# The end stage of a two-layer decoder trunk: the order of four compute engines laid out by hand, one gate half or partial product in each slot

## The chip, the cores and the metric

One NeuronCore of a Trainium2 chip runs the whole program in one launch. The metric is the device time of that launch in microseconds; the median of three runs is given. The engines are TensorE (PE, with its weight loads as PEld), VectorE (DVE), ScalarE (ACT), GpSimd (POOL) and SyncE (SP), which issues all DMAs that matter here.

## What is computed

Two pre-norm residual layers over 2048 tokens of width 1024, and a final RMSNorm. Layer 0 mixes by gated linear attention, layer 1 by dilated sliding-window attention: six heads of 128, three (window, dilation) groups each, whose outputs are combined by a softmax over their log-sum-exps. Each layer has a cross-attention into 256 memory tokens and a SiLU gate of the branch width. The end stage of the program holds the end of layer 1:

```python
    for g, (window, dil) in enumerate(DIL_GROUPS):
        ...
        o, lse = dilated_group(q, k, qkv[:, :, 2], window, dil)
    wts = jax.nn.softmax(jnp.stack(lses, axis=0), axis=0)
    o = jnp.einsum('gbth,gbthd->bthd', wts, jnp.stack(outs, axis=0).astype(jnp.float32))
...
        branch = jnp.concatenate([mix, mem_o], axis=-1) * jax.nn.silu(gate)
        x = x + branch @ w_out[i]
    return rmsnorm(x, final_norm_w)
```

## The kernel before

**Precision.** A product in float32 is made of three matmuls (`mm3`, L180 to L183): each operand is split into a high part (a cast on ACT) and a low part (the difference, on DVE or POOL), and hi x hi, hi x lo and lo x hi are summed in PSUM. The attention probabilities are split by `split_P` (L171 to L178): ACT makes the high half, POOL (L175) the low half, and SP issues a transposing DMA (L176).

**Main loop.** Layer 1 has 18 head passes (6 heads by 3 groups). The loop of `NS` = 144 slots takes eight slots a pass. In a slot s PE makes the scores of slot s - 10 (`att_scores`), the product of probabilities and values of slot s - 13 (`att_pv`, so three slots after its scores) and one 512-wide projection of q or k (`proj_t`, 24 matmuls). DVE adds the mask and takes the row maximum (L1257), ACT exponentiates (L1268). Every four slots the rotary embedding runs (`rope_a`, `rope_b`, `rope_c`: shuffle, two products, a sum, a fold, a subtraction and eight copies). Inside this loop the order of PE, DVE, ACT and POOL is the program's own (`manual_schedule` with all four engines); SP's order is always the planner's.

**Chunks of a head.** When a head's three groups are done, its statistics are transposed (`att_stats`), stored (`stats_out`), read back (`prep_load`), turned into weights (`prep_mix`, `prep_out`), read again as rows broadcast to all partitions (`item_fb`, into the tile fb), and applied to the group outputs (`item_og` loads them; `item_mul`, one DVE and two POOL products; `item_sum`, three DVE instructions). The result of a chunk of 512 tokens is one of eight 128-wide pieces of the branch, kept in DRAM (brd). The steps of the first five heads are spread over slots by `mixes`.

**End stage.** It follows the loop and has slots x = 0 to 13 and then 16 output blocks of 128 tokens. In the slots the last 10 scores and 13 value products run, the four chunks of the last gate column (`gate_half`, eight halves of 12 matmuls, then the SiLU by exponential, logarithm and exponential on ACT), the end of the fifth head, the four chunks of the sixth head (h = 5), whose piece is not stored but split into b5, and the split of w_out (four raw loads of 1 MB, `wo_split`) into wo0, wo1 and wo2. An output block multiplies the branch (seven pieces loaded and split into bhl, the eighth from b5) by w_out: `f_main` makes the seven pieces' part of one 512-wide half, P1 or P2, into a PSUM bank, `f_fin` adds the eighth, adds the residual x1 on DVE (L1651) and squares on ACT, and `f_end` applies the final norm (L1667) and stores.

In this stage only PE's order is the program's. The planner orders DVE, ACT, POOL and SP by its own estimates. Of PE's order: gate halves 0, 1 in slot 0, 2, 3 in slot 1, then one a slot to slot 5; P1 of block 0 in slot 7, of block 1 in slot 9, P2 of both in slots 11 and 12, P1 of block 2 in slot 13; all four chunks of h = 5 are loaded at x = 4, 6, 8, 10 and multiplied at x = 6, 8, 10, 12.

**PSUM.** `mm_bank` rotates over three banks (ps_mm twice, ps_x); scores have two banks (ps_g), value products one of ps_o and one of ps_tr in turn.

Of the kernel before, what the change touches and what calls it, by code (L numbers as in the profile page):

```python
# [36 lines left out]
def trunk(ctx, tc, a, out):  # L37
# [1389 lines left out]
    def mixes(s):  # L1427
# [25 lines left out]
    with ExitStack() as c5:
        c5.enter_context(tc.manual_schedule(engines={getattr(mybir.EngineType, e_) for e_ in MANUAL}))
        chunk = None
        for s in range(NS):
# [54 lines left out]
            mixes(s)  # L1511
            wcur = wnext
# [7 lines left out]
    def wo_raw(j, t):  # L1520
        SY.dma_start(t, a["w_out"][1, :, j * 256:(j + 1) * 256].rearrange("(k p) n -> p k n", p=P))
        return t

    def wo_split(raw, hi, lo):
        A.activation(out=hi, in_=raw, func=AF.Copy)
        V.tensor_tensor(out=lo, in0=raw, in1=hi.bitcast(F32), op=ALU.subtract)

    last = hds[NH - 1]
# [4 lines left out]
    def gate_half(x):  # L1533
# [7 lines left out]
        if hf == 1:  # L1541
            gate_silu(gt.pop(c), c)
# [6 lines left out]
    raws = {0: wo_raw(0, tl(stg, [P, KT, 256], F32, "stg"))}  # L1549
    wo0 = [tl(wp, WSH, F32R, "w") for _ in range(4)]  # L1550
    its, fbs, pre, b5s = {}, {}, {}, {}
    for x in range(14):
        if x < 10:
            scores(NS - 10 + x)
        if x < 13:
            pv(NS - 13 + x)
        if x == 4:
            stats_out(*att_stats(hds.pop(NH - 2), 0))
        if x < 4:
            for f in todo.pop(NS + x, []):  # L1560
                f()
            mixes(NS + x)
        if x == 7:
            f_main(fs[0], P1)
        if x == 9:
            f_main(fs[1], P1)
        for y in ((0, 1), (2, 3), (4,), (5,), (6,), (7,))[x] if x < 6 else ():
            gate_half(y)
        c, odd = divmod(x - 3, 2)
        if 0 <= c < 4 and not odd:  # L1570
            stats_out(*att_stats(last, c))
        c, odd = divmod(x - 4, 2)
        if x == 1:
            brs = [t[:, 0:(KT - 1) * P].rearrange("p (k n) -> p k n", k=KT - 1) for t in rope]
            for y in range(2):
                load_br(y)
        if 0 <= c < 4:
            if not odd:
                pre[c] = prep_load(5, c)
                its[c] = item_og(5, c)  # L1580
            else:
                prep_out(*prep_mix(pre.pop(c)))
                fbs[c] = item_fb(5, c)
        c, odd = divmod(x - 6, 2)
        if 0 <= c < 4 and not odd:
            it = its.pop(c), fbs.pop(c), last["osb"].pop(c)
            item_mul(*it)
            sg = item_sum(*it)
            b5s[c] = tl(vp, [P, 2, 512], F32R, "v")
            wo_split(sg, b5s[c][:, 0], b5s[c][:, 1])  # L1590
        if x in (1, 2):
            kh = x - 1
            wo_split(raws[0][:, 4 * kh:4 * kh + 4], wo0[kh], wo0[2 + kh])
# [3 lines left out]
        if x in (4, 5):  # L1597
            ks = slice(4 * (x - 4), 4 * (x - 3))
            wo_split(raws[1][:, ks], wo1[0][:, ks], wo1[1][:, ks])
        if x == 4:  # L1600
            raws[2] = wo_raw(2, tl(vp, [P, KT, 256], F32, "v"))
        if x == 6:
            raws[3] = wo_raw(3, tl(stg, [P, KT, 256], F32, "stg"))
        if x == 5:
            ch.close()
            f0 = c4.enter_context(pool("f0", 1, "right"))
            fp = c4.enter_context(pool("fp", 3, "right"))
            wo2 = [tl(f0, [P, KT, 512], F32R, nm) for nm in ("wh2", "wl2")]
            x1v = x1_d.rearrange("(b p) d -> b p d", p=P)
            ov = out.rearrange("(b p) d -> b p d", p=P)  # L1610
            fw = tl(wp, [P, D], F32, "w")
            SY.dma_start(fw, bcast_row(a["final_norm_w"], D))

            bhls = [tl(f0, [P, 2, KT - 1, P], F32R, f"bhl{y}") for y in range(2)]

            def load_b(p_, br=True):
                if br:
# [4 lines left out]
                return dict(p=p_, x=xt, b=bhls[p_ % 3], ss=tl(sp, [P, 4], F32, "ss4"), n=0, t={},
                            e=tl(pk, [P, D], BF16, "pm"))

            def wcol(k, lo, c0, n):
# [4 lines left out]
                return wo2[lo][:, k, c0 - 512:c0 - 512 + n]  # L1630

            def f_main(d, parts, t=None):
                t = mm_bank() if t is None else t
                d["t"][parts[0]] = t
                lo_ = parts[0][0]
                for c0, n in parts:
                    for k in range(KT - 1):
# [4 lines left out]
            def f_fin(d, parts):
                t = d["t"].pop(parts[0])
                lo_, hi_ = parts[0][0], parts[-1][0] + parts[-1][1]
                b5 = b5s[d["p"] // 4]
                ts = slice(d["p"] % 4 * P, (d["p"] % 4 + 1) * P)
                for c0, n in parts:
                    mm3(t[:, c0 - lo_:c0 - lo_ + n], b5[:, 0, ts], b5[:, 1, ts], wcol(5, 0, c0, n), wcol(5, 1, c0, n),
                        False, c0 + n == hi_)
                cs = slice(lo_, hi_)  # L1650
                V.tensor_tensor(out=d["x"][:, cs], in0=t[:, :hi_ - lo_], in1=d["x"][:, cs], op=ALU.add)  # L1651
                A.activation(out=d["e"][:, cs], in_=d["x"][:, cs], func=AF.Square,
                             accum_out=d["ss"][:, d["n"]:d["n"] + 1])
                d["n"] += 1

            def f_mm(d, parts):
                f_main(d, parts)
                f_fin(d, parts)

            def f_end(p_, d, w):  # L1660
                tot = tl(sp, [P, 1], F32, "ss")
                V.tensor_reduce(out=tot, in_=d["ss"][:, :d["n"]], axis=AX.X, op=ALU.add)
                r = rstd_of(tot, 1, D)
# [93 lines left out]
```

## Time and profile before

| What | Value |
|---|---|
| median of three runs | 2592.41 us (2585.83 to 2594.94) |
| the profiled execution's own time | 2593.54 us |
| its span | 2591.8 us |
| PE busy | 2497.6 us, 96% of the span |
| DVE, ACT, POOL busy | 1576.0, 1345.9, 582.6 us |
| first scores of the end stage | at 2332.61 us |

Times in the profile are counted from the start of the span. A row of the timeline gives the start, the duration, the engine, the line, the operation, the tile that is written and those that are read; square brackets give the idle time before the instruction and what ended it. A helper's line stands for every caller (L181 to L183 are all the split products; L1526 is the low half of every `wo_split`), so the tile names tell which product it is: ps_g<-k,q are scores, ps_o or ps_tr<-pt,v value products, ps_mm or ps_x<-h2T,w projections and gates, and products with w, q, k, wh or wl as weights and bhl, q or v as the other operand output blocks.

### The profile page before, as it was taken

The numbers are of one execution on the slowest core, as the hardware profiler recorded it, in microseconds if no ns is written. First come the engines' busy times: TensorE is split into PE (matmuls) and PEld (weight loads), VectorE is DVE, ScalarE is ACT, GpSimd is POOL, SyncE is SP. The second block draws the span as 40 slices with busy tenths as digits, with TensorE's granted clock in tenths as the row PEclk, the third lists the DMA queues.
The fourth block names the chain that finished last, engine by engine and source line by source line (L and its number), as shares of the span: only waits on it lengthen the run. The fifth ranks groups of instructions, "written<-read, shape, count | busy, mean of one in ns | idle before, by whom it ended". The sixth has DMA issues, their size and how long they took to land. (4 is left out here: it accounts for less than half of the span.)

```text
span 2591.8 us, 45023 instructions
## 1 busy us (share of the span) xinstructions
PE 2497.6 (96%) x17033; PEld 1678.4 (65%) x17033; DVE 1576.0 (61%) x3582; ACT 1345.9 (52%) x2944; POOL 582.6 (22%) x471
## 2 busy tenths in 40 slices
PE   7999999899999899999999999999999999996899
PEld 6979999788889744444544455555555555554798
DVE  7346444565875765765655455676776767677642
ACT  7346543643454545755555455565556556556222
POOL 0000000010210223455543022233232323223100
PEclk9999999899999999999999999999999999998999
DMA  6242111345544554568674314365573846659642
GB/s 211 84 130 100 62 52 74 118 109 121 155 135 125 147 171 126 152 164 188 164 200 125 118 49 115 95 176 152 140 192 101 196 122 173 153 142 250 183 153 83
DMA packets 563312, 356.55 MB, mean 138 GB/s; under 512 B 383555, under 2 KB 495637, under 8 KB 562709
## 3 DMA queue, kind: packets, MB, share of 16 engines
q1 hardware_dynamic: 563092, 353.66, 50.1%
q8 instruction: 133, 2.18, 0.4%
q14 instruction: 87, 0.70, 0.1%
HBM read 185.74 MB, written 95.86 MB: 109 GB/s over the span
## 5 line engine op out<-in xcount | busy, mean ns | idle before, releaser
L181 PE MATMUL ps_mm<-h2T,w 128*128 128x512 f16 x1112 | 422.7, 380 | 7.0 <-ACT w L851 5.7
L183 PE MATMUL ps_mm<-h2T,w 128*128 128x512 f16 x1112 | 422.4, 380 | 0.3 <-DVE w L855 0.3
L182 PE MATMUL ps_mm<-h2T,w 128*128 128x512 f16 x1112 | 422.5, 380 | 0.0
L181 PE MATMUL ps_mm<-w,hT 128*128 128x256 f16 (+1 forms) x1408 | 389.0, 276 | 3.3 <-ACT v L491 1.3
L182 PE MATMUL ps_mm<-w,hT 128*128 128x256 f16 (+1 forms) x1408 | 387.9, 276 | 0.0
L183 PE MATMUL ps_mm<-w,hT 128*128 128x256 f16 (+1 forms) x1408 | 386.5, 276 | 0.4 <-DVE hT L385 0.4
L183 PEld LDWEIGHTS <-w 128*128 128x128 f16 x1952 | 191.3, 98 | 232.4 <-issue 1.9
L181 PEld LDWEIGHTS <-w 128*128 128x128 f16 x1952 | 191.3, 98 | 217.4 <-ACT w L851 5.9
L182 PEld LDWEIGHTS <-w 128*128 128x128 f16 x1952 | 191.3, 98 | 217.0 <-issue 9.0
L175 POOL TENSOR_TENSOR ph<-pm,ph 128x512 f16<-128x512 f32 (+2 forms) x144 | 165.8, 1151 | 638.2 <-ACT ph L174 441.5
L181 PE MATMUL ps_x<-h2T,w 128*128 128x512 f16 x552 | 209.2, 379 | 1.4 <-DVE c L1079 1.4
L183 PE MATMUL ps_x<-h2T,w 128*128 128x512 f16 x552 | 209.2, 379 | 0.0
L182 PE MATMUL ps_x<-h2T,w 128*128 128x512 f16 x552 | 209.2, 379 | 0.0
L1268 ACT ACTIVATE pm<-pm,st,cols 128x256 f32<-128x256 f32 (+1 forms) x288 | 156.2, 544 | 79.8 <-DVE st L1261 78.2
L175 POOL TENSOR_TENSOR stg<-mp,stg 128x512 f16<-128x512 f32 x16 | 18.6, 1160 | 743.7 <-DMA ogd<-og 456.9
L1257 DVE CUSTOM_DVE_ANT_0 pm<-ps_g,mw 128x256 f32<-128x256 f32 (+1 forms) x288 | 93.0, 359 | 103.8 <-PE ps_g L183 103.0
L181 PEld LDWEIGHTS <-hT 128*128 128x128 f16 x1408 | 139.4, 99 | 24.7 <-issue 5.4
L182 PEld LDWEIGHTS <-hT 128*128 128x128 f16 x1408 | 139.2, 99 | 23.5 <-issue 4.5
L183 PEld LDWEIGHTS <-hT 128*128 128x128 f16 x1408 | 139.8, 99 | 18.6 <-DVE hT L385 0.7
L1217 ACT ACTIVATE rx<-rw 128x512 f16<-128x512 f32 x36 | 33.9, 941 | 115.7 <-DVE rw L1216 115.7
L1201 ACT ACTIVATE rx<-ps_mm 32x512 f32<-32x512 f32 x96 | 56.1, 584 | 58.1 <-DVE k L1227 26.1
L174 ACT ACTIVATE ph<-pm 128x512 f16<-128x512 f32 (+2 forms) x144 | 77.2, 536 | 4.5
(502 smaller groups left out, 5995.3 us busy)
## 6 DMA issues: line engine op xcount, KB each, us to landing
stg<-in_w_in_b SPq DMA_DIRECT2D x80, 256.0 KB
v<-vd SPq DMA_DIRECT2D x72, 256.0 KB
fb<-fd SPq DMA_DIRECT2D x24, 768.0 KB
od<-osb SPq DMA_DIRECT2D x68, 256.0 KB
og<-od SPq DMA_DIRECT2D x68, 256.0 KB
x<-in_x SPq DMA_DIRECT2D x32, 512.0 KB
stg<-in_w_in_b SPq DMA_DIRECT2D x24, 512.0 KB
vd<-vo SPq DMA_DIRECT2D x48, 256.0 KB
```

The source lines that it names most:

```text
L174: A.activation(out=hi, in_=src, func=AF.Copy)
L175: G.tensor_tensor(out=lo, in0=src, in1=hi, op=ALU.subtract)
L181: PE.matmul(o, sh, mh, start=first, stop=False)
L182: PE.matmul(o, sh, ml, start=False, stop=False)
L183: PE.matmul(o, sl, mh, start=False, stop=last)
L1201: A.activation(out=X[r0:r0 + 32, :], in_=t[0:32, :], func=AF.Copy)
L1217: A.activation(out=fold(X.bitcast(F16)[:, 0:512], g), in_=perm(W, g), func=AF.Copy, scale=SQ)
L1257: V.tensor_tensor_reduce(out=pm[:, at:at + w * P], in0=s[:, at:at + w * P], in1=masks["mw" if w == 2 else "mf"], scale=1.0, scalar=NEG, op ...
L1268: A.activation(out=p_, in_=p_, func=AF.Exp, scale=sc, bias=st[:, jc + jj:jc + jj + 1], accum_out=st[:, ns + jc + jj:ns + jc + jj + 1])
```

## The change

The end stage gets `manual_schedule` for PE, DVE, ACT and POOL, so that the program's order is now the order on all four. SP stays with the planner. Within this order:

- Slots 0 to 7 hold one gate half each, slots 8 to 11 P1 of blocks 0 to 3, slots 12 and 13 P2 of blocks 0 and 1. These six partial products take three banks of mm_bank, both of ps_g and ps_o.
- `gate_silu` is parted: the exponentials follow the gate's second half, the final product (`gate_out`) comes a slot later. `wo_split` is parted into `wo_hi` and `wo_lo`, the low half mostly a slot later. Statistics of h = 5 are transposed in slots 5, 7, 9, 11 and stored a slot later.
- The first raw block of w_out is asked for at the end of slot 143; its split stands in slots 0 and 1, after the rope of the loop. Raw 2 and raw 3 are loaded in slots 6 and 8 and split in slots 8, 9 and 10, 11.
- Only chunk 0 of h = 5 is handled in the slots (load 6, weights 7 and 8, product 11, sum 12). Chunk 1 is loaded in slot 12 and multiplied after block 2; chunks 2 and 3 follow in blocks 3 to 7 and 7 to 11.
- `f_end` of a block comes after P1 of the next. The split of block p + 1 (from block 4 on) stands in block p.
- Buffers: four group outputs of the last head have their own tiles (osb, rw, rx, sg2); the x1 tiles lie where q and k were; the split branch tiles lie in old v and w tiles and in a new pool; b5 lies in the staging tile.

```diff
+    def gate_e(t):
+        e = tl(bk, [P, 512], F32, "rx")
+        V.tensor_scalar(out=e, in0=t, scalar1=gneg5, scalar2=87.0, op0=ALU.mult, op1=ALU.min)
+        A.activation(out=e, in_=e, func=AF.Exp)
+        A.activation(out=e, in_=e, func=AF.Ln, bias=one1)
+        A.activation(out=e, in_=e, func=AF.Exp, scale=-1.0)
+        return e
+
+    def gate_out(t, c, e):
         sg = tl(bk, [P, 512], F32, "sg2")
-        silu(t, 512, [wg5["inv"][0]], [gneg5], sg, bk, "rx")
+        V.scalar_tensor_tensor(out=sg, in0=t, scalar=wg5["inv"][0], in1=e, op0=ALU.mult, op1=ALU.mult)
         SY.dma_start(sg_d[5][:, c * 512:(c + 1) * 512], sg)
...
             mixes(s)
+            if s == NS - 1:
+                raws = {0: wo_raw(0, tl(stg, [P, KT, 256], F32, "stg"))}
...
-    def wo_split(raw, hi, lo):
+    def wo_hi(raw, hi, lo):
         A.activation(out=hi, in_=raw, func=AF.Copy)
+
+    def wo_lo(raw, hi, lo):
         V.tensor_tensor(out=lo, in0=raw, in1=hi.bitcast(F32), op=ALU.subtract)
+    c4.enter_context(tc.manual_schedule(engines={getattr(mybir.EngineType, e_) for e_ in MANUAL}))
...
+    last["own"] = [(gk, [P, 512], F32, "osb")] + [(bk, [P, 512], F32, nm) for nm in ("rw", "rx", "sg2")]
...
+    def split_later(x, *a_):
+        wo_hi(*a_)
+        later(NS + x + 1, wo_lo, *a_)
...
     for x in range(14):
+        now[0] = x
         if x < 10:
             scores(NS - 10 + x)
         if x < 13:
             pv(NS - 13 + x)
+        for f in todo.pop(NS + x, []):
+            f()
         if x < 4:
             mixes(NS + x)
+        if x in (5, 7, 9, 11):
+            later(NS + x + 1, stats_out, *att_stats(last, (x - 5) // 2))
+        if x < 8:
+            gate_half(x)
+        elif x < 12:
+            f_main(fs[x - 8], P1, bank(ps_g) if x == 11 else None)
+        else:
+            f_main(fs[x - 12], P2, bank(ps_g if x == 12 else ps_o))
+        if x == 3:
+            later(NS + 4, stats_out, *att_stats(hds[NH - 2], 0))
+        if x == 0:
+            load_br(0)
+            load_br(1)
+        if x < 2:
+            w_split(x, 0, x)
         if x == 2:
             raws[1] = wo_raw(1, tl(stg, [P, KT, 256], F32, "stg"))
             wo1 = [tl(qp, [P, KT, 256], F32R, nm) for nm in ("q", "k")]
         if x in (4, 5):
+            w_split(x, 1, x - 4)
...
         if x == 6:
+            raws[2] = wo_raw(2, tl(stg, [P, KT, 256], F32, "stg"))
+            last_load(0)
+        if x == 6:
+            b_hi(0)
+            later(NS + 7, b_lo, 0)
+        if x == 7:
+            last_mix(0)
+            b_hi(1)
+        if x == 8:
             ch.close()
             f0 = c4.enter_context(pool("f0", 1, "right"))
...
+            b_lo(1)
+            last_out(0)
+            b_hi(2)
+            later(NS + 9, b_lo, 2)
+        if x in (8, 9):
+            w_split(x, 2, x - 8)
         if x == 10:
+            w_split(x, 3, 0)
+        if x == 9:
+            b_hi(3)
+            later(NS + 10, b_lo, 3)
+        if x == 10:
+            b5 = tl(stg, [P, 2, 2, 512], F32R, "stg")
+            xts += [t[:, y] for nm in ("q", "k") for t in (tl(qp, [P, 2, D], F32, nm),) for y in range(2)]
+            for y in range(3):
+                load_x(y)
+        if x == 11:
+            w_split(0, 3, 1)
+            for f in todo.pop(NS + 1):
+                f()
+            last_mul(0)
+        if x == 12:
+            last_sum(0, x)
+            last_load(1)
         if x == 13:
+            last_mix(1)
     for p_ in range(NB):
+        x = 14 + p_
+        d = fs[p_]
+        for f in todo.pop(NS + x, []):
+            f()
+        if 3 <= p_ < NB - 1:
+            b_hi(p_ + 1)
+        if p_ > 3:
+            f_main(d, P1)
+        f_fin(d, P1)
+        if 3 <= p_ < NB - 1:
+            b_lo(p_ + 1)
+        if p_ > 0:
+            f_end(fs.pop(p_ - 1))
+        if p_ + 1 < NB:
+            if p_ > 1:
+                f_main(d, P2)
+            f_fin(d, P2)
         else:
+            for c0 in (512, 768):
+                f_main(d, [(c0, 256)])
+                f_fin(d, [(c0, 256)])
+            f_end(d, 512)
+        if 2 < p_ + 2 < NB:
+            load_x(p_ + 2)
+        if p_ in (2, 6, 10):
+            last_mul(p_ // 4 + 1)
+        if p_ in (3, 7, 11):
+            last_sum(p_ // 4 + 1, x)
+        if p_ in (3, 7):
+            last_load(p_ // 4 + 2)
+        if p_ in (4, 8):
+            last_mix(p_ // 4 + 1)
+        if p_ in (0, 5, 9):
+            last_out(p_ // 4 + 1)
```

`last_load`, `last_mix`, `last_out`, `last_mul` and `last_sum` call the chunk steps named above for h = 5; `b_hi` and `b_lo` split a block's seven pieces, and `b_lo(p)` also asks for the pieces of block p + 2; `load_x` asks for x1 of a block; `w_split(x, j, kh)` splits half kh of raw block j, with the low half in slot x + 1.

More of the change, by code (lines that the diff above doesn't have):

```diff
@@ L1541, in gate_half @@
         if hf == 1:
-            gate_silu(gt.pop(c), c)
+            t = gt.pop(c)
+            later(NS + now[0] + 1, gate_out, t, c, gate_e(t))
     def load_br(p_):
@@ new lines, in trunk, with w_split @@
+    brs, bhs = [kp(t) for t in rope], []
+    P1, P2 = [(0, 256), (256, 256)], [(512, 512)]
+    def split_later(x, *a_):
+        wo_hi(*a_)
+        later(NS + x + 1, wo_lo, *a_)
+    def w_split(x, j, kh):
+        ks = slice(4 * kh, 4 * kh + 4)
+        if j == 0:
+            hl = wo0[kh], wo0[2 + kh]
+        elif j == 1:
+            hl = [w[:, ks] for w in wo1]
+        else:
+            hl = [w[:, ks, (j - 2) * 256:(j - 1) * 256] for w in wo2]
+        split_later(x, raws[j][:, ks], *hl)
@@ new lines, in last_load, with last_mix, last_out, last_mul @@
+    def last_load(c):
+        pre[c] = prep_load(5, c)
+        its[c] = item_og(5, c)
+    def last_mix(c):
+        pre[c] = prep_mix(pre[c])
+    def last_out(c):
+        prep_out(*pre.pop(c))
+        fbs[c] = item_fb(5, c)
+    def last_mul(c):
+        its[c] = its[c], fbs.pop(c), last["osb"].pop(c)
+        item_mul(*its[c])
+    def last_sum(c, x):
+        sg = item_sum(*its.pop(c))
+        b5s[c] = b5[:, c % 2]
+        split_later(x, sg, b5s[c][:, 0], b5s[c][:, 1])
+    x1v = x1_d.rearrange("(b p) d -> b p d", p=P)
@@ L1552, in trunk, with f_end @@
+    def f_end(d, w=D):
+        tot = tl(sp, [P, 1], F32, "ss")
+        V.tensor_reduce(out=tot, in_=d["ss"][:, :d["n"]], axis=AX.X, op=ALU.add)
+        r = rstd_of(tot, 1, D)
+        xt = d["x"]
+        for c0 in range(0, D, w):
+            cs = slice(c0, c0 + w)
+            V.scalar_tensor_tensor(out=xt[:, cs], in0=xt[:, cs], scalar=r, in1=fw[:, cs], op0=ALU.mult,
+                                   op1=ALU.mult)
+            SY.dma_start(ov[d["p"]][:, cs], xt[:, cs])
     for x in range(14):
+        now[0] = x
@@ L1556, in trunk @@
             pv(NS - 13 + x)
-        if x == 4:
-            stats_out(*att_stats(hds.pop(NH - 2), 0))
+        for f in todo.pop(NS + x, []):
+            f()
         if x < 4:
-            for f in todo.pop(NS + x, []):
-                f()
             mixes(NS + x)
[L1563 to L1593, printed above, removed]
+        if x in (5, 7, 9, 11):
[4 more added lines that the diff above has]
+            f_main(fs[x - 8], P1, bank(ps_g) if x == 11 else None)
+        else:
+            f_main(fs[x - 12], P2, bank(ps_g if x == 12 else ps_o))
[6 more added lines that the diff above has]
+            w_split(x, 0, x)
         if x == 2:
@@ L1597, in trunk @@
         if x in (4, 5):
[L1598 to L1601, printed above, removed]
+            w_split(x, 1, x - 4)
+        if x == 5:
+            hv = tl(vp, [P, 2, D], F32R, "v")
+            bhs += [[kp(hv[:, y]) for y in range(2)], [kp(tl(wp, [P, D], F32R, "w"))]]
         if x == 6:
-            raws[3] = wo_raw(3, tl(stg, [P, KT, 256], F32, "stg"))
@@ L1673, in trunk @@
[L1673 to L1683 removed]
+            bh = [tl(f0, [P, KT - 1, P], F32R, f"bh{y}") for y in range(5)]
```

141 lines of the change are left out of this document (52 added, 89 removed).

## The prediction

> **What bounds the kernel now.** I read the page's slices first, then windows over the last 260 us, then the waits of PE, then the timelines of the engines that it waits for.
>
> ```profile
> span 2591.8 us, 45023 instructions
> PE   7999999899999899999999999999999999996899
> ```
>
> A slice is 64.8 us. PE is full until the fourth slice from the end, so only the end stage can give time.
>
> ```profile
> 2332.60:2419.60 87.00, 67.08 (x449) 48.89 (x448) 62.26 (x139) 43.59 (x88) 26.80 (x18) 0.88 0.89 222
> ...
> 2439.70:2585.20 145.50, 145.50 (x961) 133.30 (x959) 60.00 (x86) 36.73 (x94) 6.98 (x4) 1.00 0.43 145
> 2332.60:2591.80 259.20, 224.34 (x1455) 191.65 (x1453) 137.70 (x256) 87.03 (x202) 37.21 (x24) 0.94 0.58 167
> ...
> PE ps_tr L1308 <- ACT pm L1268: 12.6, 3, 11.3
> PE ps_mm L181 <- DVE x L1651: 8.5, 1, 8.5
> PE ps_tr L181 <- DMA pt<-ph: 6.3, 5, 2.4
> PE ps_o L181 <- DMA pt<-ph: 0.9, 1, 0.9
> ```
>
> Columns of the windows: length, busy PE, PEld, DVE, ACT, POOL, clock, DMA share, GB/s. The first row is the fourteen slots of the end stage, the second blocks 3 to 15, where PE never rests, the third the whole stage. PE waits 28.3 us in all (12.6 + 8.5 + 6.3 + 0.9).
>
> ```profile
> 2332.61 0.22 PE L181 MATMUL ps_g<-k,q 128*128 128x128 f16 x1
> 2339.66 0.27 PE L181 MATMUL ps_g<-k,q 128*128 128x256 f16 x1
> 2340.82 0.38 PE L181 MATMUL ps_mm<-h2T,w 128*128 128x512 f16 x1
> 2346.00 0.22 PE L181 MATMUL ps_g<-k,q 128*128 128x128 f16 x1
> 2367.41 0.38 PE L1308 MATMUL ps_tr<-ident,st 128*8 128x128 f32 x1 [11.33 <-ACT pm L1268]
> 2431.59 0.79 PE L181 MATMUL ps_mm<-wh,q 128*128 128x512 f32 x1 [8.50 <-DVE x L1651]
> 2439.72 0.28 PE L181 MATMUL ps_x<-w,bhl 128*128 128x256 f32 x1
> 2473.25 0.28 PE L181 MATMUL ps_x<-w,bhl 128*128 128x256 f32 x1
> 2585.08 0.28 PE L183 MATMUL ps_mm<-wh,v 128*128 128x256 f32 x1
> ...
> 2333.77 1.23 DVE L1526 TENSOR_TENSOR w<-stg,w 128x1024 fp32r<-128x1024 f32 x1 [4.71 <-ACT w L1525]
> 2338.76 0.28 DVE L1257 CUSTOM_DVE_ANT_0 pm<-ps_g,mw 128x128 f32<-128x128 f32 x1
> 2364.94 0.42 DVE L1257 CUSTOM_DVE_ANT_0 pm<-ps_g,mw 128x256 f32<-128x256 f32 x1
> 2425.66 1.01 DVE L1386 TENSOR_TENSOR fb<-rw,fb 128x512 f32<-128x512 f32 x1 [8.14 <-DMA fb<-fd]
> 2430.87 0.67 DVE L1651 TENSOR_TENSOR x<-ps_mm,x 128x512 f32<-128x512 f32 x1
> ```
>
> Both large waits have one shape: an instruction placed too early on DVE holds what PE needs. Slot 0's scores are made at 2332.61 and read (L1257) at 2338.76; slot 3's reading is only at 2364.94, and PE's transpose of its statistics stands until 2367.41. Later item_mul of chunk 1 (L1386) sits 8.14 us for its fb load, and the residual adds that free PE's banks (L1651) stand behind it.
>
> PE's own work: 24 gate matmuls from 2340.82 to 2346.00 are 5.18 us, so a gate half is 2.59; scores and pv are 1.16 (2339.66 to 2340.82). Three blocks take 33.53 (2439.72 to 2473.25), 11.18 each. The stage needs 8 x 2.59 + 10 x 1.16 + 3 lone pv at about 0.5 + 5 transposes at about 0.17 + 16 x 11.18 = 213.6 us, and 6.7 from the last matmul (2585.08) to the end. It takes 259.2, so 38.9 are to be had: 28.2 of waits and 10.7 of a low clock, that is 0.38 us of slow matmuls for each us waited. A stage without waits ends at 2332.6 + 213.6 + 6.7 = 2552.9.
>
> **The change, part by part.** Its arithmetic is the same; the blocks' work merely shifts (four P1 and two P2 instead of three and two before block 0).
>
> *Gone.* The 8.50: chunk 1's load, sums and split move behind blocks 0 to 3, and the six banks' adds stand ahead of them. It comes back as at most 1 us: item_mul(1) then follows block 2, PE having only 1.4 us of work in each of blocks 0 and 1 and about 6.2 in block 2, so DVE waits there some 4 us for fb and b_lo(4) is about 1 late. Chunks 2 and 3 have a block of 11.18 for each step. The 11.33 goes in its old form: statistics now have a slot of their own.
>
> *New: strict order on DVE, ACT and POOL.* What the planner interleaved is now in sequence. Slot -1 (s = 143) ends with item_mul, then the last rope, and only then comes slot 0's score reading.
>
> ```profile
> 2329.02 2.62 SPq L1377 DMA_DIRECT2D fb<-fd  x1
> ...
> 2351.06 0.62 SPq L1377 DMA_DIRECT2D fb<-fd  x1
> ...
> 2357.72 1.02 DVE L1386 TENSOR_TENSOR fb<-og,fb 128x512 f32<-128x512 f32 x1 [2.76 <-DMA fb<-fd]
> ...
> 2340.59 1.27 POOL L1384 TENSOR_TENSOR fb<-og,fb 128x512 f32<-128x512 f32 x1
> 2341.81 1.52 POOL L1389 TENSOR_TENSOR fb<-og,fb 128x512 f32<-128x512 f32 x1
> 2343.29 1.27 POOL L1211 TENSOR_TENSOR rw<-rw,rope 128x512 f32<-128x512 f32 x1
> ...
> 2317.36 0.47 DVE L1227 COPY q<-rx 32x512 f16<-32x512 f16 x2
> ```
>
> An fb load lands 6.0 us after its issue (2351.68 to 2357.72), so that of 2331.64 lands near 2337.6. In order POOL then needs 1.27 + 1.52 + 1.27 = 4.1, to 2341.7. DVE adds, ACT folds, DVE subtracts (three 512-wide instructions at about the 0.67 of L1651's row, 1.9 in all) and DVE makes eight copies (four pairs of 0.47, 1.9): 2345.5. Slot 0's scores are read by 2346.3, seven us later than now. ps_g has two banks, so slot 2's scores need that reading. PE gets there at 2332.6 + 0.6 (its present wait) + 2 x 3.75 = 2340.7 (a slot is 1.16 + 2.59), and stands **5.5 us**. If fb is there in time, this falls to about 1; if the planner issues it later, it grows by as much.
>
> *The chain from scores to pv, three slots long.*
>
> ```profile
> 2366.08 0.60 ACT L1268 ACTIVATE pm<-pm,st,cols 128x256 f32<-128x256 f32 x1 [0.16 <-DVE st L1261]
> 2367.39 0.63 ACT L174 ACTIVATE ph<-pm 128x512 f16<-128x512 f32 x1
> 2368.09 1.15 POOL L175 TENSOR_TENSOR ph<-pm,ph 128x512 f16<-128x512 f32 x1 [3.96 <-ACT ph L174]
> ...
> 2379.60 1.70 SPq L176 DMA_TRANSPOSE pt<-ph  x1
> ...
> 2382.62 0.29 PE L181 MATMUL ps_tr<-pt,v 128*128 128x128 f16 x1 [2.41 <-DMA pt<-ph]
> ...
> 2386.33 6.68 DMA pt<-ph
> ...
> 2363.87 0.63 ACT L304 ACTIVATE rx<-rx 128x512 f32<-128x512 f32 x1 [0.73 <-DVE rx L302]
> 2365.29 0.63 ACT L306 ACTIVATE rx<-rx 128x512 f32<-128x512 f32 x1
> ```
>
> Reading to exponentials 1.1 (2364.94 to 2366.08), exponentials 1.3, high half 0.6, POOL 1.2, issue 1.3 to 1.7, landing 1.3 (2381.30 to 2382.62): 7.0 from the reading, against 11.3 for three slots. So slots whose reading isn't late cost nothing. Late are three. Slot 0's, read from 2345.5: its pv in slot 3 at about 2352, wait 1.2. Slot 3's, behind item_mul of the last h = 4 chunk, which stands for fb until 2357.7 again: slot 6 waits 1.8. Slot 4's, behind that chunk's sum (three 512-wide DVE instructions, some 2.2) and a gate's three passes on ACT (2363.87 to 2365.92): slot 7 waits 2.6. Then last_mix(0) on DVE waits for statistics stored only a slot earlier; b_lo(1) stands behind it, and block 1's P1 in slot 9 waits about 1.5. Sum with the 0.6, the 5.5 and the 1.0: **14.2 us** of waits; I hold 7 to 21 possible.
>
> *Clock.* At 0.38 a microsecond, 14.2 cost 5.4; the slow stretch after slot 2 is partly hidden under slot 3's wait (1.2), so 4; bounds 0 and 5.4.
>
> ```profile
> 2367.40:2374.00 6.60, 6.59 (x31) 3.87 (x32) 3.43 (x10) 2.85 (x7) 1.15 (x1) 0.64 0.61 161
> 2382.00:2388.00 6.00, 5.38 (x37) 5.26 (x38) 6.00 (x13) 5.16 (x10) 2.15 (x2) 0.72 0.72 217
> ```
>
> The windows after the waits of 11.33 and of 2.41 were granted 0.64 and 0.72. [...]
>
> *DMA.* SP's queue isn't laid out by hand. The loads of x1 move from slots 6, 7 and 10 to 10, raws 2 and 3 from 4 and 6 to 6 and 8, og and sg of chunks 1 to 3 out of the slots; raws 0 and 1, br and the h = 4 items stay between slots -1 and 4, where the DMA share is already 0.89. A transpose landed 1.3 us after issue at 2381.30, but the one issued at 2386.33, with rope and x loads ahead, 6.68 after the start of its issue. Two such delays of 5 in slots 3 to 5 are possible; I take 3.5, bounds 0 and 10.
>
> *Neutral.* New tiles for bhs and b5, f_end one block later: DVE is 60.0 of 145.5 busy in the block stage, ACT 36.7, so both hide; uncovered, f_end's scaling of 1024 elements would cost about twice L1651's 0.67 a block. The last block's drain keeps its parts.
>
> Sum: 2552.9 + 14.2 + 4 + 3.5 = 2574.6 of span. The profiled run took 2593.54 for a span of 2591.8 (1.74 beside it), 1.13 over the median of 2592.41: 2574.6 + 1.74 - 1.13 = **2575**.
>
> **Rivals.** *PE-bound* (0.15): only slot 0's 0.6 and slot 2's 5.5 remain, with 2.3 of clock: 2552.9 + 8.4 + 0.6 = 2562. For it: DVE is busy 62 of 87 us. Against: every wait above has its row.
>
> *Chain-bound* (0.14): the longest chain seen, 2332.61 to a pv of slot 3 at about 2352.8, holds in every slot, 20.2 / 3 = 6.7 for 3.75: 8 x 2.95 = 23.6, with 3.1 of other waits and 10 of clock: 2590, no measurable change. This is also the case in which the hand-made order doesn't do what it says, since SP still decides when transposes go.
>
> *The clock stays low* (0.08): short waits in each of slots 0 to 9 keep the clock at half. PE's work there, 8 x 3.75 + 2 x 6.06 = 42.1 (P1 without its last k is 7/16 of 11.18, 4.9, and 1.16), doubles; with the 0.6 and 5.5 that is 2552.9 + 48.2 + 0.6 = 2602, slower. It decides once the idle of a slot recurs at 2.4 us, the wait after which 0.72 was granted. Against: the present stage, with more idle, holds 0.88. [...]
>
> **How the numbers follow.** Forecast 0.63, own range 2562 to 2585 (waits 7 to 21, DMA, clock). What a measurement of this kernel can tell is about 0.3%, 7.8 us: faster is below 2584.6 (forecast and PE-bound, 0.78), same is chain-bound (0.14), slower the clock (0.08). The range, 2558 to 2592, leaves out the clock case and edges of the others.
>
> **What would show it.** Right: no L1651 wait over 2 us after slot 13; slot 2's scores waiting about 5 us for DVE L1257; L1257 of slot 0 after the copies (L1227); slots 0 to 7 together 42 to 50 us; blocks still 11.18. Wrong: slot 2 doesn't wait (fb landed early or rope isn't late); pv waits in each slot, near 3 us (chain-bound); a clock under 0.7 through slots 3 to 9; block 0's fin waiting for b5 of chunk 0, or DVE standing over 5 us at item_mul(1).

## The result and the profile after

| | before | after | ratio, 95% interval |
|---|---|---|---|
| first set of runs | 2587.69 us | 2572.10 us | 0.9936 [0.9914, 0.9958] |
| second | 2589.64 us | 2571.69 us | 0.9930 [0.9917, 0.9942] |
| third | 2589.81 us | 2572.12 us | 0.9929 [0.9917, 0.9941] |

The change makes the kernel 0.7% faster, 16 to 18 us. 2575 was forecast. The profiled execution of the changed kernel took 2568.94 us, for a span of 2567.2.

The page of the changed kernel, its span and the row of PE in 40 slices (64.2 us each):

```profile
span 2567.2 us, 45017 instructions
...
PE   7989999899999999999999999999999999998999
```

The 6 of before in the fourth slice from the end is an 8, and the 8 behind it a 9; the end stage lies in these last slices. The same windows view as before, of the changed kernel (length, busy PE, PEld, DVE, ACT, POOL, clock, DMA share, GB/s): slots 0 to 7, slots 8 to 13 with the first blocks, the whole stage.

```profile
2330.00:2374.20 44.20, 35.10 (x221) 19.95 (x220) 38.29 (x79) 25.84 (x56) 17.03 (x13) 0.88 0.87 212
...
2374.20:2430.00 55.80, 55.16 (x390) 50.21 (x388) 39.98 (x74) 22.18 (x50) 10.56 (x7) 1.00 0.80 229
...
2330.00:2567.20 237.20, 220.33 (x1455) 188.51 (x1453) 136.66 (x250) 83.62 (x196) 33.36 (x24) 0.97 0.60 179
```

Nearly all that is left to win stands in the first row. From slot 8 on PE is busy 55.16 of 55.80 us. In slots 0 to 7 it rests for 9.1 us of 44.2, at a clock of 0.88, while DVE is busy 38.29 of the 44.2 and the DMA engines 0.87. The next view is what PE waited for over the stage (us in total, times, longest):

```profile
PE ps_tr L181 <- DMA pt<-ph: 5.7, 2, 5.2
PE ps_o L181 <- DMA pt<-ph: 2.5, 1, 2.5
PE ps_tr L1308 <- DVE osb L1297: 0.9, 1, 0.9
PE ps_mm L181 <- ACT stg L1535: 0.7, 1, 0.7
PE ps_g L181 <- DVE mx L1257: 0.4, 1, 0.4
PE ps_mm L183 <- DVE stg L1538: 0.2, 1, 0.2
```

They sum to 10.4 us, where 28.3 were. Both large waits of before are gone, and what remains are mostly transposed probabilities that land late. (Line numbers have moved: the residual add L1651 is now L1650, the weight split L1525 and L1526 is L1535 and L1538.)

PE's timeline of the changed kernel gives the stage's length and the place of each wait (start, duration, then the instruction; idle time and its releaser in brackets):

```profile
2330.01 0.22 PE L181 MATMUL ps_g<-k,q 128*128 128x128 f16 x1
...
2341.80 0.27 PE L181 MATMUL ps_g<-k,q 128*128 128x256 f16 x1 [0.38 <-DVE mx L1257]
2347.86 0.26 PE L181 MATMUL ps_tr<-pt,v 128*128 128x128 f16 x1 [5.25 <-DMA pt<-ph]
...
2360.22 0.23 PE L181 MATMUL ps_o<-pt,v 128*128 128x128 f16 x1 [2.53 <-DMA pt<-ph]
2361.84 0.27 PE L1308 MATMUL ps_tr<-ident,st 128*8 128x128 f32 x1 [0.94 <-DVE osb L1297]
...
2374.15 0.27 PE L181 MATMUL ps_g<-k,q 128*128 128x256 f16 x1
...
2437.41 0.28 PE L181 MATMUL ps_x<-w,w 128*128 128x256 f32 x1
...
2470.85 0.28 PE L181 MATMUL ps_x<-w,v 128*128 128x256 f32 x1
```

The first row is slot 0, the row at 2374.15 slot 8: eight slots in 44.1 us. The stage runs from 2330.01 to the end at 2567.2, 237.2 us, where 259.2 were (2332.61 to 2591.8). So of the 24.6 us by which the two spans differ, 22.0 belong to the stage: 17.9 are waits (28.3 less 10.4), and the other 4.1 are nearly all low clock: the same 1455 matmuls kept PE busy for 224.34 us before, at a granted 0.94, and for 220.33 now, at 0.97. The remaining 2.6 are the earlier start of the stage, after a loop that the change leaves as it was. Such a shift comes and goes between executions: in the profiles of this study slot 0 starts anywhere from 2330.0 to 2339.1. For this reason the length of the stage, not the span, is compared below. The profiled execution of before was 5.9 us above the median of its set (2593.54 against 2587.69) and that of the changed kernel 3.2 below (2568.94 against 2572.10), so these two profiles show more gain than the 16 to 18 us of the medians. The kernel before has only one profile, and how much its stage varies is not known.

Three blocks take 33.44 us (2437.41 to 2470.85), 11.15 each.

### The profile page after: what moved, and what is told of

The parts are those of the page before. It is cut to its first block, busy times and chain, and to the rows that moved or that the text cites. A ratio compares the mean times of both kernels' runs of the same rounds, so it can differ in the third digit from the quotient of the medians.

```text
span 2567.2 us, 45017 instructions
## 1 busy us (share of the span) xinstructions
PE 2489.6 (97%) x17033; PEld 1673.3 (65%) x17033; DVE 1579.0 (62%) x3582; ACT 1345.7 (52%) x2944; POOL 579.2 (23%) x471
## 4 chain that ended last, share of the span: by engine, by line
PE 79%; DVE 6%; DMA 5%; issue 4%; ACT 4%; POOL 2%; SPq 1%; DVEq 0%; POOLq 0%; ACTq 0%
PE ps_mm L181 15%; PE ps_mm L183 15%; PE ps_mm L182 15%; PE ps_x L181 6%; PE ps_x L182 6%; PE ps_x L183 6%; DMA mpt<-stg 1%; PE ps_o L183 1%; PE ps_o L181 1%; PE ps_o L182 1%; PE ps_g L181 1%; PE ps_g L182 1%; PE ps_g L183 1%; DMA h2T<-stg 1%; PE ps_tr L168 1%
## 5 line engine op out<-in xcount | busy, mean ns | idle before, releaser
L1257 DVE CUSTOM_DVE_ANT_0 pm<-ps_g,mw 128x256 f32<-128x256 f32 (+1 forms) x288 | 93.0, 359 | 99.6 <-PE ps_g L183 99.0
L183 PEld LDWEIGHTS <-hT 128*128 128x128 f16 x1408 | 139.2, 99 | 17.9 <-DVE hT L385 0.7
L1201 ACT ACTIVATE rx<-ps_mm 32x512 f32<-32x512 f32 x96 | 56.1, 584 | 57.8 <-PE ps_mm L183 24.6
```

The costliest lines, as they stand in the source:

```text
L183: PE.matmul(o, sl, mh, start=False, stop=last)
L1201: A.activation(out=X[r0:r0 + 32, :], in_=t[0:32, :], func=AF.Copy)
L1257: V.tensor_tensor_reduce(out=pm[:, at:at + w * P], in0=s[:, at:at + w * P], in1=masks["mw" if w == 2 else "mf"], scale=1.0, scalar=NEG, op ...
```

## What slots 0 to 7 do now

The prediction let slot 0's scores be read on DVE after the rope's copies, so that slot 2 would wait. DVE's timeline of the changed kernel:

```profile
2332.14 1.03 DVE L1386 TENSOR_TENSOR fb<-og,fb 128x512 f32<-128x512 f32 x1 [3.08 <-DMA fb<-fd]
2333.07 0.29 DVE L1257 CUSTOM_DVE_ANT_0 pm<-ps_g,mw 128x128 f32<-128x128 f32 x1
...
2336.30 1.24 DVE L1396 TENSOR_TENSOR fb<-fb 128x512 f32<-128x512 f32 x1
...
2338.07 1.40 DVE L1397 TENSOR_TENSOR fb<-fb 128x512 f32<-128x512 f32 x1
...
2340.96 0.43 DVE L1257 CUSTOM_DVE_ANT_0 pm<-ps_g,mw 128x256 f32<-128x256 f32 x1
...
2345.00 1.35 DVE L1227 COPY k<-rx 32x512 f16<-32x512 f16 x2
```

Slot 0's reading (L1257 at 2333.07) stands right behind item_mul (L1386), and slot 1's (2340.96) in the middle of the rope, ahead of the copies (L1227). The program's text has it otherwise. The main loop and the end stage each open a hand order of their own; within each the order is strict, but at the seam the planner wove the first instructions of the second list into the last ones of the first. So slot 2's scores did not wait, and slot 3's waited 0.38 us.

What does wait is slot 3's value product, 5.25 us. SP's timeline of the changed kernel shows why (start and duration of the issue):

```profile
2337.49 2.57 SPq L1299 DMA_DIRECT2D od<-osb  x1
2340.16 2.63 SPq L1561 DMA_DIRECT2D rope<-brd  x4
2342.90 1.24 SPq L176 DMA_TRANSPOSE pt<-ph  x1
...
2351.52 0.38 SPq L1462 DMA_DIRECT2D stg<-in_w_out  x1
2353.40 1.21 SPq L176 DMA_TRANSPOSE pt<-ph  x1
```

POOL has the low half of slot 0's probabilities ready at 2338.92 (its row is shown at the end), but SP first issues a store of a head's output and the four loads of br, and gets to the transpose at 2342.90. That is 4.0 us of queue; the transpose then lands 3.7 us after the end of its issue, at 2347.86. For slot 5 the transpose of 2353.40 goes out behind a 1 MB load of w_out and lands 5.6 us after the end of its issue, at 2360.22; PE waits 2.53. SP could not have issued it sooner, because POOL has that low half ready only at 2353.37: slot 2's scores are made from 2337.50 on, but DVE reads them at 2347.12, behind the rope, a low half of w_out and a gate's first pass, and ACT starts their exponentials at 2350.14, behind that gate's three passes and a cast of w_out. So in the compute engines' own order, too, something stands ahead of what PE needs. The clock falls behind both, as the windows of the changed kernel after the two waits show:

```profile
2348.80:2353.00 4.20, 4.20 (x16) 1.64 (x15) 3.36 (x6) 3.02 (x7) 1.02 (x1) 0.64 1.04 260
2361.90:2366.40 4.50, 4.50 (x15) 1.81 (x15) 3.20 (x8) 4.44 (x12) 1.16 (x1) 0.62 0.71 232
```

Granted 0.64 and 0.62: from its first start to its last end a gate half took 4.25 and 4.44 us there and 2.76 in slot 7, so 3.2 us are lost. The first window follows an idle time of 5.25 us, the second idle times of only 2.53 and 0.94, with 0.7 us of work between them; its gate half lost no less (1.7 us against 1.5). Behind the 2.41 wait of before the clock was 0.72.

## Experiments

All start from the changed kernel. The table gives the stage by one profile each, and the median time of all executions. "Slots 0 to 7" is the time from slot 0's to slot 8's first scores, "from slot 8" that from there to the end of the span.

| kernel | slots 0 to 7 | from slot 8 | stage | PE's waits | median us | ratio to before |
|---|---|---|---|---|---|---|
| changed kernel | 44.1 | 193.1 | 237.2 | 10.4 | 2572.10 | 0.9936 [0.9914, 0.9958] |
| again | 43.4 | 193.0 | 236.4 | 8.8 | 2571.69 | 0.9930 [0.9917, 0.9942] |
| third time | 45.5 | 193.6 | 239.1 | 10.8 | 2572.12 | 0.9929 [0.9917, 0.9941] |
| planner's order | 48.4 | 206.7 | 255.1 | 24.7 | 2588.04 | 0.9993 [0.9983, 1.0002] |
| one list | 46.3 | 194.8 | 241.1 | 12.4 | 2572.97 | 0.9934 [0.9919, 0.9949] |
| chunk 1 early | 44.4 | 205.2 | 249.6 | 20.4 | 2581.04 | 0.9970 [0.9958, 0.9981] |
| SP by hand too | 46.0 | 201.4 | 247.4 | 18.4 | 2582.11 | 0.9971 [0.9955, 0.9986] |
| br later | 45.2 | 194.0 | 239.2 | 12.2 | 2574.70 | 0.9949 [0.9935, 0.9962] |
| br and raw 1 later | 45.4 | 193.7 | 239.1 | 12.9 | 2578.76 | 0.9957 [0.9944, 0.9969] |
| low halves of raw 0 out | 44.9 | 197.7 | 242.6 | 14.4 | 2576.01 | 0.9942 [0.9930, 0.9955] |
| low halves of raw 0 twice | 46.2 | 192.4 | 238.6 | 11.6 | 2573.67 | 0.9933 [0.9921, 0.9946] |
| item_mul on DVE | 42.2 | 195.1 | 237.3 | 9.9 | 2572.41 | 0.9931 [0.9918, 0.9945] |
| br later and item_mul on DVE | 44.3 | 193.6 | 237.9 | 9.8 | 2573.39 | 0.9930 [0.9918, 0.9943] |

The first three rows are one and the same kernel: its stage moves by 2.7 us between profiles, and by 2.1 in slots 0 to 7 alone.

**Is it the order, or the new layout and slots?** The line that makes the stage's order the program's on DVE, ACT and POOL is taken out; buffers, slots and the parting of steps stay.

```diff
-    c4.enter_context(tc.manual_schedule(engines={getattr(mybir.EngineType, e_) for e_ in MANUAL}))
```

> The changed kernel without its one line that lays out DVE, ACT and POOL by hand in the end stage: the new slots, buffers and six early partials stay, the planner orders the three engines. If the hand order carries the gain, the planner again puts work that waits for DMAs ahead of what PE needs: PE waits over 20 us in the stage and the time is within 8 us of the kernel before (2580 to 2596). If the new slots carry it (chunk 1 behind block 0, one gate half a slot, statistics with a slot of their own), the waits stay near the changed kernel's 10 us and the time at 2567 to 2578.

Nothing of the gain is left: 0.9993 [0.9983, 1.0002]. PE's waits over the stage of this kernel, and SP's timeline in its later slots:

```profile
PE ps_tr L181 <- DMA pt<-ph: 18.0, 3, 7.2
PE ps_mm L181 <- DVE q L1649: 2.9, 1, 2.9
```

```profile
2392.95 2.68 SPq L1612 DMA_DIRECT2D q<-x1d  x2
...
2398.42 2.05 SPq L176 DMA_TRANSPOSE pt<-ph  x1
...
2403.30 1.96 SPq L176 DMA_TRANSPOSE pt<-ph  x1
```

The planner again puts splits of w_out ahead of readings of scores, residual adds late (2.9 us for L1649) and x1 loads ahead of transposes; value products in slots 3, 4 and 11 wait 3.79, 7.02 and 7.22 us. So the layout by itself brings nothing that can be measured in the time, and the hand order on top of it brings all. The order on the old layout was not tried: there b5's tiles, v and raw 2 share two buffers, and by the code a strict order would let an instruction wait for one that stands behind it. The layout is what permits the order; that is argued, not shown.

**Is the seam the reason why slot 2 did not wait?** Loop and stage are put in one list.

```diff
-        c5.enter_context(tc.manual_schedule(engines={getattr(mybir.EngineType, e_) for e_ in MANUAL}))
+        c4.enter_context(tc.manual_schedule(engines={getattr(mybir.EngineType, e_) for e_ in MANUAL}))
...
-    c4.enter_context(tc.manual_schedule(engines={getattr(mybir.EngineType, e_) for e_ in MANUAL}))
```

> The changed kernel with the main loop and the end stage in one list instead of two, so that DVE, ACT and POOL keep the program's order across the seam too. The prediction assumed this: then DVE reads slot 0's scores only after the loop's last rope copies, slot 2's scores wait 4 to 7 us for L1257, and the stage is 2 to 6 us longer than the changed kernel's. If the seam is not what kept slot 2 from waiting (the fb load just came earlier), slot 2's wait stays under 1.5 us and the time is the changed kernel's.

DVE's and then PE's timeline of this kernel, whose stage starts at 2332.07:

```profile
2333.98 1.02 DVE L1386 TENSOR_TENSOR fb<-og,fb 128x512 f32<-128x512 f32 x1 [2.77 <-DMA fb<-fd]
...
2342.82 0.49 DVE L1227 COPY k<-rx 32x512 f16<-32x512 f16 x2
...
2343.40 0.28 DVE L1257 CUSTOM_DVE_ANT_0 pm<-ps_g,mw 128x128 f32<-128x128 f32 x1
```

```profile
2344.08 0.27 PE L181 MATMUL ps_g<-k,q 128*128 128x128 f16 x1 [4.36 <-DVE mx L1257]
```

Now slot 0's scores are read after the last copy, and slot 2's scores wait 4.36 us: the step that the prediction described, in the order that it assumed. That the size is so near has luck in it. The fb load was there 1.9 us after slot 0's start (L1386 at 2333.98) and not 5.0, a case for which the prediction let the wait fall to about 1; but from there to the reading it took 9.4 us (to 2343.40) where the prediction counted 7.9. The waits sum to 12.4 (14.2 forecast) and the stage is 241.1 us. Yet the time is that of the changed kernel within both intervals. The 4.36 is not added to the others: slot 3's value product, which waited 5.25, now finds its transpose there, and slot 4's waits 0.70.

**Was the 8.50 us wait really the place of chunk 1?** Chunk 1's output and product go back to slot 13, ahead of the first residual adds.

```diff
         if x == 13:
             last_mix(1)
+            last_out(1)
+            last_mul(1)
...
-        if p_ in (2, 6, 10):
+        if p_ in (6, 10):
...
-        if p_ in (0, 5, 9):
+        if p_ in (5, 9):
```

> The changed kernel with the weights and the product of chunk 1 (last_out, last_mul) moved from blocks 0 and 2 to slot 13, ahead of block 0's adds. If the 8.5 us of the kernel before was DVE standing at item_mul for fb with the adds behind it, DVE waits here 8 to 11 us for fb at L1386, PE then waits 6 to 9 us before P2 of block 2, runs slow after it, and the stage is 7 to 13 us longer than the changed kernel's. If the banks of the six partials give cover enough, PE waits under 2 us and the time does not change.

DVE's and PE's timeline of this kernel:

```profile
2427.32 1.01 DVE L1386 TENSOR_TENSOR fb<-rw,fb 128x512 f32<-128x512 f32 x1 [6.20 <-DMA fb<-fd]
2428.26 0.68 DVE L1650 TENSOR_TENSOR q<-ps_mm,q 128x512 f32<-128x512 f32 x1
```

```profile
2428.99 0.80 PE L181 MATMUL ps_mm<-wh,bh 128*128 128x512 f32 x1 [6.84 <-DVE q L1650]
```

It is back in its old form: item_mul stands 6.20 us for fb, the adds stand behind it, PE stands 6.84 us for its bank, and the matmul takes 0.80 where from 2434.11 on it takes 0.40. All of the stage's loss lies from slot 8 on (205.2 us against 193); 2.9 us of it are a wait of slot 10's value product that this edit does not explain. The median is 9 us over the changed kernel's: this one move carries about half of the change's gain.

**Would a hand order of SP help?** SP joins the list.

```diff
-    c4.enter_context(tc.manual_schedule(engines={getattr(mybir.EngineType, e_) for e_ in MANUAL}))
+    c4.enter_context(tc.manual_schedule(engines={getattr(mybir.EngineType, e_) for e_ in MANUAL + ("SP",)}))
```

> The changed kernel with SP's order laid out by the program too in the end stage. If the remaining waits come from where the planner puts the transposes in SP's queue, they fall: slots 3 and 5 wait under 3 us together instead of 7.8, and the time is 3 to 8 us less than the changed kernel's. If a strict SP queue stands for data (fb, og, statistics) with transposes behind it, pv waits grow, to 15 us or more in all, and the time is 5 us or more above the changed kernel's.

SP's and PE's timeline of this kernel:

```profile
2331.71 8.59 SPq L176 DMA_TRANSPOSE pt<-ph  x2
...
2351.18 6.16 SPq L176 DMA_TRANSPOSE pt<-ph  x2
```

```profile
2358.85 0.26 PE L181 MATMUL ps_tr<-pt,v 128*128 128x128 f16 x1 [10.10 <-DMA pt<-ph]
```

SP now issues everything in the text's order. Between the two transposes of the first row it stands 6.1 us for slot 0's probabilities, with the loads of the next steps behind it. They go out from 2343.72 to 2351.07, and so ahead of slot 1's transpose: its operand is ready on POOL at 2346.12, it is issued at 2351.18, and it lands at 2358.85. That value product waits 10.1 us. The program's text is good for the engines that compute, but it names DMAs before their data are ready. Leaving SP to the planner is worth about 10 us here.

**The changed kernel again.**

> The changed kernel once more, as the measure for the two runs beside it: 2566 to 2579 us, and the same two waits of PE, about 5 us in slot 3 and 2 to 3 us in slot 5.

> The changed kernel once more, beside the run with both edits on the same chip: 2570 to 2574 us, a stage of 236 to 238 us with 8 to 11 us of PE's waits, slot 3's wait for its transpose at 4 to 5 us the largest.

The same three places wait each time: slot 3's value product 4.16 and 4.26 us, slot 5's 1.35 and 2.62, slot 5's statistics 2.14 and 1.65.

**Is it SP's queue that holds slot 3?** The br loads, which stand ahead of slot 0's transpose, go to slot 3 (two columns of each tile are set to zero first, so that the load cannot be issued earlier).

```diff
-        if x == 0:
+        if x == 3:
+            for t in rope:
+                G.memset(t[:, 639:641], 0.0)
             load_br(0)
             load_br(1)
```

> The changed kernel with the loads of the branch pieces of blocks 0 and 1 (four DMAs) held back until slot 3; a write of two columns into each tile on POOL makes them wait and is overwritten by the loads. If slot 3's wait of 5.25 us comes from these four standing ahead of slot 0's transpose in SP's queue, the transpose is issued some 4 us earlier, the wait falls under 2 us, the slow clock after it goes, and the time is 3 to 7 us less than the changed kernel's. If the transfers in flight decide (fb, od, og ahead of it), the wait stays over 3 us; if the next late link takes its place, slot 3's wait goes and slots 4 to 6 wait longer by as much, and the time changes by under 2 us.

SP's timeline of this kernel, its slot 0 starting at 2333.69, and PE's:

```profile
2344.08 2.04 SPq L176 DMA_TRANSPOSE pt<-ph  x1
```

```profile
2348.34 0.22 PE L181 MATMUL ps_tr<-pt,v 128*128 128x128 f16 x1 [1.83 <-DMA pt<-ph]
...
2361.71 0.29 PE L181 MATMUL ps_o<-pt,v 128*128 128x128 f16 x1 [3.80 <-DMA pt<-ph]
2365.37 0.37 PE L1308 MATMUL ps_tr<-ident,st 128*8 128x128 f32 x1 [2.52 <-DVE osb L1297]
```

The transpose of slot 0 goes out 10.4 us after the slot's start (2344.08 less 2333.69) instead of 12.9, and slot 3's wait falls from 5.25 to 1.83. So the place in the queue was most of its cause. But slot 4 now waits 1.27, slot 5 3.80 and 2.52, and slots 0 to 7 are no shorter: 45.2 us. In the next kernel the load of raw 1 moves behind slot 2's transpose as well:

```diff
+        if x == 2:
+            raw1 = tl(stg, [P, KT, 256], F32, "stg")
+            G.memset(raw1[:, :, 0:2], 0.0)
+            raws[1] = wo_raw(1, raw1)
...
-            raws[1] = wo_raw(1, tl(stg, [P, KT, 256], F32, "stg"))
```

> As the run before, and the load of the second 1 MB of w_out held back until POOL has the low half of slot 2's probabilities (a write of two columns, overwritten by the load), so that slot 2's transpose is issued ahead of it. If this megabyte is what made that transpose land 5.6 us after its issue, slot 5's wait falls from 2.5 to under 1 us and the time is 5 to 9 us less than the changed kernel's. If the block then arrives too late for its split in slot 4, ACT stands for it and the waits reappear in slots 6 to 8: no gain beyond the run before.

The same again: the value products wait 0.3 to 1.8 us each, but slot 5's statistics wait 5.07 for DVE's L1297, and the sum is 12.9. Slot 5's transpose, now ahead of the 1 MB load, lands 1.3 us after the end of its issue (2364.01 to 2365.35) and not 5.6; so that load had made it late. Its median is 6 to 7 us over the changed kernel's although its stage is as long as the third profile's; its slot 0 started at 2339.05, the latest of all. Why is open.

**Is DVE's list the bound in slots 0 to 6?** It is busy 38.29 of 44.2 us there. Two kernels take two low halves of w_out (1.2 us each on DVE) out of it and put two more in:

```diff
+        if j == 0:
+            wo_hi(raws[j][:, ks], *hl)
+            G.memset(hl[1].bitcast(F32), 0.0)
+            return
```

> The changed kernel with the low halves of w_out's first 256 columns set to zero on POOL instead of computed on DVE: two subtractions of 1.2 us leave DVE's list in slots 1 and 2, and the products with these halves add nothing to the output. If DVE's list is what slots 0 to 6 run at (28.1 us busy in the 29.6 from 2332.1 to 2361.7), the waits of PE in slots 2 to 6 fall by 2 to 3 us and with the clock the stage is 2 to 4 us shorter than the changed kernel's 237. If the transposes' way through SP and the DMA rings decides, waits and stage stay within 1 us.

```diff
+        if j == 0:
+            later(NS + x + 1, wo_lo, raws[j][:, ks], *hl)
```

> The changed kernel with the same two subtractions made twice: 2.4 us more on DVE in slots 1 and 2, the result the same. If DVE's list is the bound there, PE's waits grow by 2 to 3 us and the stage by 2 to 4. If not, both stay within 1 us.

Taken out, slots 0 to 7 last 44.9 us, inside the range of the changed kernel's three profiles (43.4 to 45.5); its stage is longer by later waits of value products, up to 2.25 us, which this edit does not explain. It is not a clean test, though. The zeros are two POOL instructions of 0.95 us, and DVE stood 2.95 us for the second fb, whose load went out 16.3 us after slot 0's start instead of 13.9 to 14.8.

Put in twice, the slots last 46.2, 0.7 over the range, and the time stays (2573.67). But PE's largest wait is now for DVE's L1297, the copy that frees ps_tr, in slot 5. DVE's and PE's timeline of this kernel:

```profile
2338.79 1.02 DVE L1386 TENSOR_TENSOR fb<-og,fb 128x512 f32<-128x512 f32 x1 [3.15 <-DMA fb<-fd]
```

```profile
2370.16 0.37 PE L1308 MATMUL ps_tr<-ident,st 128*8 128x128 f32 x1 [5.72 <-DVE osb L1297]
```

It is 31.4 us from DVE's first product behind the first fb to this transpose of slot 5's statistics, and DVE is busy for 29.95 of them. In the changed kernel it is 29.7 (2332.14 to 2361.84, 28.13 busy), and 29.3 and 29.5 in its other two profiles; with br later, and with br and raw 1 later, 29.3 both times. In all of these PE's transpose waits for L1297. So DVE's list, nearly without a rest, sets when PE gets past slot 5's statistics: whatever wait is removed ahead of it, PE waits for L1297 instead (0.94, then 2.52, then 5.07). Two more passes of 1.2 us each make this stretch 1.7 to 2.1 longer, which is too little for the median to tell. A third kernel takes work from POOL, beside whose L1389 DVE's L1396 took 2.01 us (at 2354.64 in the changed kernel's trace) and 0.68 with POOL idle (at 2471.66):

```diff
-        h, c, sg, og = it
+        (h, c, sg, og), G = it, V if it[0] == 4 and it[1] > 1 else nc.gpsimd
```

> The changed kernel with the POOL products of the last two h = 4 chunks (four of 1.3 to 2.0 us) made on DVE. DVE instructions beside these products took longer in the changed kernel's trace (L1396 2.01 for 0.69, L1261 1.26 for 0.23, L1397 1.69 for 0.69). If that overlap costs DVE more than the four products do (about 1.0 each, 4 in all), DVE's stretch of slots 0 to 5 gets 1 to 3 us shorter and the stage with it. If the four products cost more than the overlap, the stage gets 1 to 4 us longer.

42.2 us, 1.2 under the range, but 195.1 from slot 8 on and no change of the time. The stretch from DVE's first product to slot 5's statistics takes 29.2 us: without POOL's products beside it, DVE gains about what the four products cost it. The last one makes both edits that had an effect in these slots:

> Both edits at once: the load of br moved from slot 0 to slot 3, and chunk 2's and 3's products of item_mul for h = 4 on DVE in place of POOL. Theory that two bounds take turns (SP's order first, POOL beside DVE behind it): each edit alone only hands its wait to the other, together they shorten slots 0 to 6: PE's waits in the stage fall from 8.8 to 10.4 us to about 5, the stage from 236.8 to 232 to 234 us, the time to about 2568. Rival, that the waits are kept up by the whole of the transfers and chains of these slots and only change their place: waits of 8 to 12 us again, the stage at 236 to 240 us, the time at 2571 to 2576.

PE's waits over the stage of this kernel, the largest:

```profile
PE ps_g L181 <- DVE mx L1257: 2.9, 3, 1.4
PE ps_o L181 <- DMA pt<-ph: 2.2, 2, 1.6
PE ps_tr L1308 <- DVE osb L1297: 1.9, 1, 1.9
```

The sum is 9.8 us as before; it is only spread over more places. The theory that SP's order and POOL beside DVE take turns falls; the stretch of DVE is 29.1 us here, as before. So in slots 0 to 5 it is DVE's list that keeps up the sum of the waits when one of them is removed; SP's br loads and POOL's products are excluded as the one cause. That a shorter list alone would help is not shown: with the low halves out, slot 5's statistics did not wait for DVE and yet were transposed only 32.6 us after slot 0's start, where the changed kernel has 31.1 to 32.0. The transposes and the second fb come nearly as late. No version is measurably faster than the changed kernel.

## Why the prediction held, step by step

The forecast of 2575 was near, but its largest single wait, in slot 2, did not come: of its own signs, "slot 2 doesn't wait" stood under wrong, and came.

**The size of the stage without waits** (213.6 + 6.7 = 220.3 us). The measured stage is 237.2 = 220.3 + 10.4 of waits + 6.5. Of the 6.5 some 3.2 are the low clock of the two windows. The rest, about 3, is mostly work counted too short, in small amounts: slot 8 took 6.36 us (2374.15 to 2380.51), for 6.06 in the count. The blocks, at 11.15, were right. The same shortfall stood in the price of 0.38 us of slow matmuls for each us waited: with about 3 of the 10.7 taken off, it is 0.27 as an estimate, and 3.2 for 10.4 is 0.31.

**The 8.50, "gone, back as at most 1".** Right, and shown by putting chunk 1 back. Block 4 waits 0.68 and 0.22 us for its b5. The 11.33 is gone as well: of the transposes of statistics only slot 5's waits, 0.94 us, and for a copy on DVE. The 4 us that DVE was to stand at item_mul(1) did not come: its timeline has that instruction without a wait, between two residual adds.

```profile
2420.62 1.79 DVE L1386 TENSOR_TENSOR fb<-rw,fb 128x512 f32<-128x512 f32 x1
```

**"Strict order on DVE, ACT and POOL: only then comes slot 0's score reading", 5.5 us for slot 2.** This is the step that failed. It took the two hand orders for one list. They are two, the planner weaves them together at the seam, and slot 2 did not wait at all. In one list the wait is there with 4.36 us, so the mechanism was right, and by luck nearly the size, for an order that the kernel does not have. That the time is the same in both says that the term should not have been added to the late slots behind it: when slot 2 waits, slot 3 does not.

**The chain: 1.2, 1.8, 2.6, 1.5 for slots 3, 6, 7 and 9.** Right in kind, late transposes, but wrong in place and size: 5.25 in slot 3, 2.53 and 0.94 in slot 5, nothing in slots 6, 7 and 9, and 0.48 in slot 11. **DMA, 3.5 for transposes behind bulk loads in slots 3 to 5.** This is what was seen there: in the two rows of SP's queue, 4.0 us of queue and landings of 3.7 and 5.6 us where 1.3 was the short one. The two terms are one wait, counted in two steps: chain and DMA together 10.6, measured 8.7, of which 0.94 is the wait for DVE's copy. In all, 14.2 of waits and 3.5 of DMA were forecast, and 10.4 measured.

**Clock, 4.** 3.2, at a granted 0.62 to 0.64. Behind the 5.25 a gate half lost 1.5 us (4.25 for 2.76), behind the 2.53 and 0.94 another lost 1.7 (4.44 for 2.76). So the sum came near the forecast's 4, but the loss did not grow with the wait, as a price for each us would have it.

From slot 0 on, 242.0 us were forecast (2574.6 less 2332.6), and 237.2, 236.4 and 239.1 were measured. So the forecast of the stage was 3 to 6 us too long, and nearer than its worst term, because a wait that isn't there (5.5) and a count too short (about 3) have opposite signs. That the time came within 3 us of the forecast is partly luck.

**The rivals.** PE-bound (2562) fails: it had 6.1 us of waits, in slots 0 and 2, and 10.4 came, in other places. Chain-bound (2590) fails in size, since only two or three slots wait, but its sentence on SP was right: what is left over is set in SP's queue and the landings behind it, and in DVE's list. The clock that stays low (2602) did not come: 0.88 in slots 0 to 7 and 1.00 from 2374.20 to 2430.00. The half clock that it counts with is seen for short stretches only: behind the 5.25 and behind the 0.94 the first gate matmuls start 0.43 us apart, for about 3 us each time, and the later ones 0.22. That the change does not do what it says was true at the seam only.

## What to carry to other kernels

A load's consumer must not stand on an engine ahead of the instruction that frees the matrix engine's banks; moving one chunk's weights and product behind the first blocks was worth about half of this change (9 us of 16 to 18), and a planner that goes by its own estimates did not find it. Here a hand order paid on the engines that compute, and the DMA queue did better with the planner (by 10 us), because the text names transfers before they can start. Before you add up late slots, ask whether one wait swallows the next, and look for an engine whose list has no rest under all of them: removing single waits here mostly moved them to the end of DVE's list, and the sum stayed at 9 to 14 us.

## What the runs showed of the hardware

Some DVE instructions took longer beside POOL than with POOL idle. Two rows of POOL in the changed kernel:

```profile
2335.70 1.29 POOL L1211 TENSOR_TENSOR rw<-rw,rope 128x512 f32<-128x512 f32 x1
2337.69 1.23 POOL L175 TENSOR_TENSOR ph<-pm,ph 128x384 f16<-128x384 f32 x1 [0.69 <-ACT ph L174]
```

They end at 2336.99 and 2338.92; DVE's L1396 (2336.30, 1.24 us) and L1397 (2338.07, 1.40) end at 2337.54 and 2339.47, each 0.55 us later. With POOL idle they took 0.68 and 0.69 us in the same trace (2471.66 and 2472.44), and L1396 took 0.68 with one list. It looks as if DVE stood until POOL was done and then did most of its work; the rows show the times, not the cause. L1297 (2335.70) took 0.68 us beside the first of the two rows, as it did at 2361.01 with POOL idle.
